# A sixth two-level product (M5), inner results as chains of sums in PSUM, and more weight splits on GpSimd, in a two-level Strassen MLP kernel

## The chip, the cores and the metric

The kernel runs on one core of one Trainium2 chip. The time is device time in microseconds (us), the median of several executions. The core has a tensor engine (TensorE, "PE" in the profile; "PEld" is its weight load), VectorE ("DVE"), ScalarE ("ACT"), GpSimd ("POOL"), SyncE ("SP"), which only issues transfers here, and 16 DMA engines. One profiled execution of each kernel gives the trace. Unless it is said otherwise, runs compared below are fast runs (the granted TensorE clock of the two main profiles is 0.99 or more).

## The reference

```python
# x: 8 x 1024 x 1024, w1: 1024 x 4096, w2: 4096 x 1024, all float32
h = x @ w1
h = 0.5 * h * (1 + np.tanh(np.sqrt(2 / np.pi) * (h + 0.044715 * h ** 3)))
return (h @ w2).astype(np.float32)
```

## The kernel before

The 8192 rows of x are worked on in eight super-blocks of 1024, SB0 to SB7. Each has two stages. "M-one" is x @ w1 with the GELU, as one level of Strassen-Winograd: seven products instead of eight, 448 matmuls of 512 columns, in float16 with float32 sums in PSUM. "M-two" is the second matmul, again seven products M1 to M7. Their operands are differences of blocks of g (the GELU's result) and sums of blocks of w2.

In SB0 and SB1 the sums of w1 and w2 are still being made, on chip, mostly by VectorE, and written to DRAM. From SB2 on they are loaded. There, M-two uses a second level: in the kernel before, M1, M2, M3, M6 and M7 are each seven smaller products (class `Inner`), and M4 and M5 stay one-level. A one-level product takes 64 matmuls of 512 columns, a two-level one 112 of 256.

The smaller products need their own weight sums, "splits". They are made once, during SB1 and SB2, either by VectorE (`split_jobs`) or by GpSimd (`split_on_pool`):

```python
def split_on_pool(m, h):                  # GpSimd: half h of product m's splits
    raw = []
    for k in range(2):
        raw.append(unit(2, HALF))         # a buffer of pool `up`
        nc.sync.dma_start(out=flat(raw[k]), in_=stored(w2_d[2*k+h], raw2_d[2*k+h], m))
    t = {}
    for n, (_, u, op, v) in W_SUMS.items():           # four sums
        if n % 2:
            two = unit(2, HALF)
        t[n] = two[:, (n + 1) % 2]
        ...
        nc.gpsimd.tensor_tensor(out=t[n], in0=in0, in1=in1, op=op)
        nc.gpsimd.dma_start(out=in_d[m][...], in_=t[n])
...
# in M-one, after block c of 16:
if sb == 2 and c < 8 and c % 2 == 0:
    split_on_pool(FROM_SUMS[c // 4], c // 2 % 2)      # FROM_SUMS = (1, 3)
```

So before, GpSimd makes splits only in SB2's M-one; M2's are made by VectorE in SB1's M-two.

The inner products are put together by VectorE, mostly with one copy and then sums that read PSUM:

```python
def steps(self, into):                    # class Inner; ab, bb, cb are PSUM banks
    self.multiply(1, ab, True);  act_copy(v, ab);              yield 1
    self.multiply(6, bb, True);  tt(c12, pair(v), pair(bb), ADD, True); ...; yield 2
    self.multiply(2, ab, False); act_copy(c11, pair(ab)); ...; yield 3
    self.multiply(7, bb, False); tt(c21, pair(v), pair(bb), ADD, True); ...; yield 4
    ...                                   # products 5, 4, 3
```

Work of VectorE that belongs to other products is put into slots of the PE sequence by a table, `FILL_2`: "27:a34 d21 d12" means that after step 7 of M2 three jobs are issued ("a" makes an operand, "x" a block difference, "d" and "e" are sums of outputs). The program pins these jobs of VectorE to their order, so a job that waits holds up those behind it (e4_fill below shows a stand of 5.23 us).

Two pools matter: `up` has 26 buffers of 4 KB per partition for everything (weights, differences, results), `gcp` has 4 for operands. A new tile gets the buffer that came free, and its first writer waits for that buffer's last reader.

## Time and profile before

| | before |
|---|---|
| time, median of 3 runs | 1528.55 us (1527.73 to 1528.93) |
| PE busy | 1517.1 of 1525.9 us (99%) |
| SB1: M-one, M-two | 96.91, 96.69 us |
| SB2: M-one, M-two | 96.82, 88.76 us |
| SB3 to SB6, each: M-one, M-two | 96.7, 88.75 us |

Stages are counted here and below from the first matmul of a stage to the first matmul of the next. First the page of the profile of before: its span and the busy time of each engine.

```profile
span 1525.9 us, 22990 instructions
PE 1517.1 (99%) x8702; PEld 852.3 (56%) x8702; DVE 1073.8 (70%) x1354; ACT 486.3 (32%) x817; POOL 357.2 (23%) x380
```

Next the chain of waits, that is the chain of work that ended last, in order of time, for SB3: start, duration, engine and line. Line 366 is M-one, 791 a one-level product of M-two, 726 the two-level ones.

```profile
594.78 96.69 PE ps L366 x448
691.48 13.81 PE ps L791 x64
705.29 36.68 PE ps L726 x336
741.97 13.81 PE ps L791 x64
755.78 24.45 PE ps L726 x224
```

PE waits for nobody here. A one-level product takes 13.81 us, a two-level one 36.68 / 3 = 12.23 us. The waits of PE in before, with total, number and longest in us:

```profile
PE ps L366 <- DVE tmp L142: 1.5, 2, 1.4
PE ps L366 <- DVE u L142: 1.4, 1, 1.4
...
PE ps L366 <- ACT tmp L430: 0.6, 1, 0.6
```

With the one line left out (1.2 us at the very start) they sum to 4.7 us, all before SB1's M-one is 4 us old. The kernel is bound by PE alone, and a new wait of PE has nothing to hide behind.

### The profile page before, as it was taken

The numbers are of one execution on the slowest core, as the hardware profiler recorded it, in microseconds if no ns is written. First come the engines' busy times: TensorE is split into PE (matmuls) and PEld (weight loads), VectorE is DVE, ScalarE is ACT, GpSimd is POOL, SyncE is SP. The second block draws the span as 40 slices with busy tenths as digits, with TensorE's granted clock in tenths as the row PEclk, the third lists the DMA queues.
The fourth block names the chain that finished last, engine by engine and source line by source line (L and its number), as shares of the span: only waits on it lengthen the run. The fifth ranks groups of instructions, "written<-read, shape, count | busy, mean of one in ns | idle before, by whom it ended". The sixth has DMA issues, their size and how long they took to land.

```text
span 1525.9 us, 22990 instructions
## 1 busy us (share of the span) xinstructions
PE 1517.1 (99%) x8702; PEld 852.3 (56%) x8702; DVE 1073.8 (70%) x1354; ACT 486.3 (32%) x817; POOL 357.2 (23%) x380
## 2 busy tenths in 40 slices
PE   9999999999999999999999999999999999999999
PEld 4444444444444677446764477544875448744486
DVE  5876868768755787557875587656876567855786
ACT  6655024410144212442124411344113441144300
POOL 1242011211297022130212203131121400204011
PEclk9999999999999999999999999999999999999999
DMA  9999985894998899769996699966999769993697
GB/s 317 348 327 349 253 281 184 281 304 156 351 362 232 309 324 312 240 159 328 321 305 212 176 348 320 312 186 198 329 308 325 185 211 320 306 353 90 221 326 185
DMA packets 226191, 417.84 MB, mean 274 GB/s; under 512 B 78752, under 2 KB 85920, under 8 KB 225184
## 3 DMA queue, kind: packets, MB, share of 16 engines
q1 hardware_dynamic: 193536, 314.64, 61.4%
q0 software_dynamic: 32544, 101.73, 24.4%
q8 instruction: 68, 1.11, 0.3%
q14 instruction: 43, 0.35, 0.1%
HBM read 311.43 MB, written 119.54 MB: 282 GB/s over the span
## 4 chain that ended last, share of the span: by engine, by line
PE 85%; DVE 0%; issue 0%
PE ps L366 44%; PE ps L726 24%; PE ps L791 17%; DVE u L142 0%
## 5 line engine op out<-in xcount | busy, mean ns | idle before, releaser
L366 PE MATMUL ps<-u 128*128 128x512 f16 x3584 | 776.1, 379 | 3.6 <-DVE tmp L142 1.5
L366 PEld LDWEIGHTS <-u 128*128 128x128 f16 x3584 | 350.5, 98 | 427.1 <-issue 4.7
L142 DVE TENSOR_TENSOR tmp<-tmp,ps 128x512 f32<-128x512 f32 x528 | 361.7, 686 | 298.1 <-ACT tmp L430 114.6
L376 ACT ACTIVATE g<-tmp 128x512 f16<-128x512 f32 x256 | 161.1, 630 | 294.4 <-DVE tmp L142 294.3
L726 PE MATMUL ps<-u,gc 128*128 128x256 f16 x1920 | 224.3, 273 | 0.0
L142 DVE TENSOR_TENSOR u<-u 128x2048 f16<-128x2048 f16 (+3 forms) x233 | 211.9, 937 | 16.6 <-ACT u L321 11.7
L791 PE MATMUL ps<-u,gc 128*128 128x512 f16 x1024 | 222.6, 379 | 0.0
L726 PEld LDWEIGHTS <-gc 128*128 128x128 f16 x1920 | 187.9, 98 | 21.7
L376 ACT ACTIVATE g<-ps 128x512 f16<-128x512 f32 x256 | 151.4, 596 | 88.1 <-PE ps L366 87.9
L791 PEld LDWEIGHTS <-gc 128*128 128x128 f16 x1024 | 100.1, 98 | 119.6
L791 PE MATMUL ps<-u,g 128*128 128x512 f16 x640 | 139.8, 379 | 0.0
L490 POOL DMA_DIRECT2D out_dram<-u x58 | 58.5, 1019 | 311.2 <-DVE u L142 299.0
L142 DVE TENSOR_TENSOR u<-u,ps 128x512 f32<-128x512 f32 x131 | 89.7, 685 | 46.1 <-PE ps L791 17.0
L158 ACT COPY tmp<-ps 128x512 f32<-128x512 f32 x54 | 31.6, 585 | 272.1 <-PE ps L726 161.3
L469 POOL TENSOR_TENSOR u<-g,g 128x2048 f16<-128x2048 f16 x24 | 97.2, 4067 | 75.0 <-ACT g L376 60.1
L791 PEld LDWEIGHTS <-g 128*128 128x128 f16 x640 | 62.7, 98 | 75.5
L726 PE MATMUL ps<-u,g 128*128 128x256 f16 x864 | 103.1, 273 | 0.0
L478 POOL DMA_DIRECT2D out_dram<-u x52 | 39.0, 770 | 249.0 <-ACT u L158 227.3
L430 ACT COPY tmp<-ps 128x512 f32<-128x512 f32 x128 | 72.9, 569 | 69.7 <-PE ps L366 69.7
L142 DVE TENSOR_TENSOR tmp<-ps,tmp 128x512 f32<-128x512 f32 x128 | 88.3, 690 | 5.9 <-PE ps L366 1.2
L726 PEld LDWEIGHTS <-g 128*128 128x128 f16 x864 | 84.5, 98 | 11.1
L142 DVE TENSOR_TENSOR u<-tmp,ps 128x512 f32<-128x512 f32 x60 | 41.3, 688 | 63.9 <-PE ps L726 41.4
(42 smaller groups left out, 736.2 us busy)
## 6 DMA issues: line engine op xcount, KB each, us to landing
u<-w_d SPq DMA_DIRECT2D x384, 256.0 KB, 7.2
u<-in_d SPq DMA_DIRECT2D x120, 512.0 KB, 7.3
u<-raw_d SPq DMA_DIRECT2D x132, 256.0 KB, 6.6
out_dram<-u POOLq DMA_DIRECT2D x58, 512.0 KB, 9.0
u<-raw_d SPq DMA_DIRECT2D x56, 512.0 KB, 7.1
gc<-in_w_dram SPq DMA_DIRECT2D x48, 512.0 KB, 6.5
w_d<-u POOLq DMA_DIRECT2D x36, 512.0 KB, 4.2
raw_d<-u SPq DMA_DIRECT2D x32, 512.0 KB, 9.9
```

What stands on the lines that cost most here:

```text
L142: i = nc.vector.tensor_tensor(out=out, in0=in0, in1=in1, op=op)
L158: tc.keep_in_program_order(nc.scalar.copy(out=out, in_=in_))
L366: nc.tensor.matmul(bank, lhsT=ops[:, k, :], rhs=xs[m][:, k, :], start=(first and k == 0), stop=(k == KH - 1), skip_group_check=not first,)
L376: gelu_last[0] = nc.scalar.activation(out=g[b][:, c, :], in_=src, func=GELU)
L430: nc.scalar.copy(out=v, in_=pb)
L469: nc.gpsimd.tensor_tensor(out=early[m][b], in0=gu, in1=gv, op=SUB)
L478: return nc.gpsimd.dma_start(out=out2[r0:r0 + P, o0:o0 + OH], in_=src, **kw)
L490: return nc.gpsimd.dma_start(out=rows, in_=src, **kw)
L726: tc.keep_in_program_order(nc.tensor.matmul(bank[:, i * OH // 2:(i + 1) * OH // 2], lhsT=t[:, c, i * P:(i + 1) * P], rhs=self.y[j][:, c, : ...
L791: i = nc.tensor.matmul(pair(bank), lhsT=a[:, c, :], rhs=chunks(pieces[c // QC])[:, :, c % QC, :], start=(first and c == 0), stop=(c == NI ...
```

## The change

M5 becomes two-level as well, which takes PE work away. To have VectorE carry it, the inner results are rewritten: products 1, 6, 7 and 4 add up in one PSUM bank, and after each of the four ScalarE copies the sum so far into the result; VectorE adds the rest. Output block 12, which is M3 + M5 and was added by an accumulating store, is added on chip ("f" jobs). The splits of M2 and M5 are made by GpSimd in SB1's M-one. GpSimd's splits take their buffers from `gcp` now and no longer from `up`, in SB1 and in SB2, and SB2's are spread over blocks 0, 3, 6 and 9 instead of 0, 2, 4 and 6. GpSimd also makes two more block differences (M6's, `EARLY`) at the end of each M-one from SB2 on. Left out of the cuts below: a turned sign in the fourth weight sum, and differences that are now written over one of their operands.

```diff
-FROM_2 = (2,)
-FROM_SUMS = (1, 3)
-INNER = MADE_INNER + FROM_2 + FROM_SUMS
+ON_POOL = {1: (2, 5), 2: (1, 3)}
+INNER = MADE_INNER + ON_POOL[1] + ON_POOL[2]
...
-EARLY = ((1, "11"), (1, "21"), (2, "11"), (2, "21"))
-W_ORDER = (1, 6, 2, 7, 5, 4, 3)
+EARLY = ((1, "11"), (1, "21"), (2, "11"), (2, "21"), (6, "11"), (6, "21"))
+W_ORDER = (1, 2, 6, 5, 7, 3, 4)
...
-    ;12:a21;14:a22;15:a23;17:a24
-    ;21:u0 u1;22:a31;23:u2 u3;24:a32;25:a33 d11;26:d22;27:a34 d21 d12
-    ;32:g50;34:g51 e11;35:g52 e22;36:e21;37:g53 e12
-    ...
+    ;11:x522;13:a21;14:a22;15:a23;16:a24;17:x521
+    ;21:u0 u1;23:a31 u2;24:a32;25:a33;26:a34;27:u3 x511
+    ;31:x512;32:d11;33:a51;34:a52;35:a53;36:a54;37:d22 d21 d12
+    ;51:e11 e22;53:a61 e21;54:a62;55:a63;56:a64;57:e12 x721
+    ...
-            if sb == 2 and c < 8 and c % 2 == 0:
-                split_on_pool(FROM_SUMS[c // 4], c // 2 % 2)
+            if sb in ON_POOL and c < 12 and c % 3 == 0:
+                split_on_pool(ON_POOL[sb][c // 6], c // 3 % 2)
...
-        if sb:
-            for m in FROM_2:
-                for job in split_jobs(m, lambda: pieces(m)):
-                    job()
...
-            raw.append(unit(2, HALF))
+            raw.append(gcp.tile([P, 2, HALF], DT, name="gc"))
...
-                two = unit(2, HALF)
+                two = gcp.tile([P, 2, HALF], DT, name="gc")
...
-            self.multiply(1, ab, True)
-            v = temp()
-            act_copy(v, ab)
-            ...
+            for n, (j, bank, first, out, adds) in enumerate((
+                (1, a, True, "11", ()),
+                (2, b, True, None, ("11",)),
+                (6, a, False, "12", ()),
+                (5, c, True, None, ("12",)),
+                (7, a, False, "22", (("22", c),)),
+                (3, b, True, None, ("12",)),
+                (4, a, False, "21", ()),
+            ), 1):
+                self.multiply(j, bank, first)
+                if out is not None:
+                    t = quarter(into, out)
+                    if self.base is None:
+                        act_copy(t, pair(bank))
+                    else:
+                        tt(t, quarter(self.base, out), pair(bank), ADD, True)
+                for o in adds:
+                    ...
+                    tt(t, t, pair(ps), ADD, True)
+                ...
+                yield n
...
-            3: Inner(3, g, out("12")),
-            6: Inner(6, g, out("22", accum_op=ADD)),
+            3: Inner(3, g),
+            5: Inner(5, g),
+            6: Inner(6, g, out("22", accum_op=ADD), x=early[6]),
...
+                elif kind == "m":
+                    add(u2, 5, b, SUB)
+                    ...
+                elif kind == "f":
+                    add(into[3], 5, b, ADD)
+                    if b in ("22", "12"):
+                        store_rows(sb, "12", a, into[3][a])
```

Product 6 adds onto bank a, so it may not start before ScalarE has copied bank a after product 1. Only product 2 (16 matmuls, 1.75 us) lies between, so a copy that is late by more than about 1 us stops PE.

More of the change, by code (lines that the diff above doesn't have):

```diff
@@ L65 @@
 W_TERMS = {1: "11", 2: "21", 3: "22"}
-W_SUMS = {1: (5, "12", SUB, "11"), 2: (6, "22", SUB, 1), 3: (7, "22", SUB, "12"), 4: (4, 2, SUB, "21")}
+W_SUMS = {1: (5, "12", SUB, "11"), 2: (6, "22", SUB, 1), 3: (7, "22", SUB, "12"), 4: (4, "21", SUB, 2)}
 S_TERMS = {1: "11", 2: "12", 4: "22"}
 S_SUMS = {1: (5, "21", ADD, "22"), 2: (6, 1, SUB, "11"), 3: (7, "11", SUB, "21"), 4: (3, "12", SUB, 2)}
-EARLY = ((1, "11"), (1, "21"), (2, "11"), (2, "21"))
-W_ORDER = (1, 6, 2, 7, 5, 4, 3)
+EARLY = ((1, "11"), (1, "21"), (2, "11"), (2, "21"), (6, "11"), (6, "21"))
+W_ORDER = (1, 2, 6, 5, 7, 3, 4)
 def slots(table):
     return {(int(k[0]), int(k[1])): v.split() for k, v in (row.split(":") for row in table.split(";"))}
-FILL_2 = slots("""00:x122 x112 a11 a12 a13 a14 x222 x212 x622 x612 x621 x611
-    ;12:a21;14:a22;15:a23;17:a24
-    ;21:u0 u1;22:a31;23:u2 u3;24:a32;25:a33 d11;26:d22;27:a34 d21 d12
-    ;32:g50;34:g51 e11;35:g52 e22;36:e21;37:g53 e12
-    ;50:a61 x721;51:a62 x722;52:a63 x711;53:a64 x712
-    ;64:a71;66:a72;67:a73;71:a74;72:n5;73:n1;74:n2;75:n7;76:n6""".replace("\n    ", ""))
+FILL_2 = slots("""00:x122 x112 a11 a12 a13 a14 x222 x212 x622 x612
+    ;11:x522;13:a21;14:a22;15:a23;16:a24;17:x521
+    ;21:u0 u1;23:a31 u2;24:a32;25:a33;26:a34;27:u3 x511
+    ;31:x512;32:d11;33:a51;34:a52;35:a53;36:a54;37:d22 d21 d12
+    ;51:e11 e22;53:a61 e21;54:a62;55:a63;56:a64;57:e12 x721
+    ;61:x722 x711;62:x712 m11;63:a71;64:a72;65:a73 m22;66:a74;67:m21 m12
+    ;71:f11 f12;72:f21 f22;73:n5;74:n1;75:n2;76:n7;77:n6""".replace("\n    ", ""))
 @with_exitstack
@@ L279, in __init__, with make @@
             self[3], self[4] = blocks["11"], blocks["22"]
-        def make(self, *ms, cols=slice(None), pin=False):
+        def make(self, *ms, cols=slice(None), pin=False, over=False):
             for m in ms:
@@ L284, in make @@
                 if m not in self:
-                    self[m] = unit(KH, HT)
+                    self[m] = self.blocks[u] if over and m in IN_PLACE else unit(KH, HT)
                 tt(self[m][:, :, cols], self.blocks[u][:, :, cols], self.blocks[v][:, :, cols], SUB, pin)
@@ L387, in matmul1 @@
         xb = [None]
-        early = {1: {}, 2: {}}
+        early = {1: {}, 2: {}, 6: {}}
         blocks = None
@@ L464, in matmul1 @@
                     x_transpose(xb[0], load_in_order, blocks, range((c - 9) // 2, (c - 7) // 2))
-            if sb > 1 and c >= NI - 4:
-                m, b = EARLY[c - NI + 4]
-                early[m][b] = unit(NI // 2, HT // 2)
+            if sb > 1 and c >= NI - len(EARLY):
+                m, b = EARLY[c - NI + len(EARLY)]
                 gu, gv = (inner_block(g[t], b) for t in A_TERMS[m])
+                early[m][b] = gu if m in IN_PLACE else unit(NI // 2, HT // 2)
                 nc.gpsimd.tensor_tensor(out=early[m][b], in0=gu, in1=gv, op=SUB)
@@ L597, in prepare @@
             ops[i] = operand2(g, m, q, True)
-        fill = [lambda m=m: xs.make(m, pin=True) for m in (5, 1, 2, 7, 6)]
+        fill = [lambda m=m: xs.make(m, pin=True, over=True) for m in (5, 1, 2, 7, 6)]
         if sb:
@@ L735, in steps @@
         def steps(self, into):
-            base = self.base
-            c11, c12, c21, c22 = (quarter(into, b) for b in ("11", "12", "21", "22"))
-            if base is not None:
-                b11, b12, b21, b22 = (quarter(base, b) for b in ("11", "12", "21", "22"))
-            ab, bb, cb = psum(), psum(), psum()
-            self.multiply(1, ab, True)
-            v = temp()
-            act_copy(v, ab)
-            yield 1
-            self.multiply(6, bb, True)
-            tt(c12, pair(v), pair(bb), ADD, True)
@@ L748, in steps @@
-            if base is not None:
-                tt(c12, c12, b12, ADD, True)
-            yield 2
-            self.multiply(2, ab, False)
-            if base is None:
-                act_copy(c11, pair(ab))
-            else:
-                tt(c11, b11, pair(ab), ADD, True)
-            self.part("11", c11)
-            yield 3
-            self.multiply(7, bb, False)
-            tt(c21, pair(v), pair(bb), ADD, True)
-            if base is not None:
-                tt(c22, c21, b22, ADD, True)
-                tt(c21, c21, b21, ADD, True)
@@ L763, in steps @@
-            yield 4
-            self.multiply(5, cb, True)
-            tt(c22, c21 if base is None else c22, pair(cb), ADD, True)
-            self.part("22", c22)
-            yield 5
-            self.multiply(4, ab, True)
-            tt(c21, c21, pair(ab), SUB, True)
-            self.part("21", c21)
-            self.rows(1, into[1])
-            yield 6
-            self.multiply(3, cb, False)
-            tt(c12, c12, pair(cb), ADD, True)
-            self.part("12", c12)
-            self.rows(0, into[0])
@@ L777, in steps @@
-            yield 7
+            a, b, c = psum(), psum(), psum()
+            for n, (j, bank, first, out, adds) in enumerate((
[15 more added lines that the diff above has]
+                for o in adds:
+                    o, ps = o if isinstance(o, tuple) else (o, bank)
+                    t = quarter(into, o)
+                    tt(t, t, pair(ps), ADD, True)
+                for o, at in (("11", 2), ("22", 5), ("12", 6), ("21", 7)):
+                    if n == at:
+                        self.part(o, quarter(into, o))
+                if n > 5:
+                    self.rows(n - 6, into[n - 6])
+                yield n
@@ L821, in matmul2 @@
         end = sb == NSB - 1
-        ops, pieces = {}, {}
         u2, u = halves()
@@ L838, in matmul2 @@
             products[7] = Inner(7, g, out("11", accum_op=ADD))
-        def copy(q, ps):
-            t = temp()
-            act_copy(t, ps)
-            return t
         def post4(q, ps):
@@ L847, in post4, with add @@
             store(sb, "21", q, u[q])
-        def post5(q, ps):
-            store(sb, "12", q, copy(q, ps), accum_op=ADD)
-            tt(u[q], u[q], ps, SUB, True)
-            if not end:
-                store(sb, "11", q, u[q])
-        posts = {4: post4, 5: post5}
-        def load(m):
-            if m in products:
-                products[m].load()
-            else:
-                pieces[m] = load_pieces(m)
+        def add(o, m, b, op):
+            t = quarter(o, b)
+            tt(t, t, quarter(into[m], b), op, True)
         def run(key):
             for job in FILL_2.get(key, ()):
-                kind, m, i = job[0], int(job[1]), job[2:]
+                kind, b = job[0], job[1:]
+                m, i, a = int(b[0]), b[1:], int(b[0]) - 1
                 if kind == "x":
@@ L869, in run @@
                     products[m].make(int(i))
-                elif kind == "g":
-                    ops[m, int(i)] = operand2(g, m, int(i), True)
                 elif kind == "u":
                     tt(u[m], u[m], rows[1][m], ADD, True)
-                elif kind in "de":
-                    b = job[1:]
-                    d = quarter(into[1], b)
-                    tt(d, d, quarter(into[2 if kind == "d" else 3], b), SUB if kind == "d" else ADD, True)
-                    if job in ("e21", "e12"):
-                        a = int(b[0]) - 1
-                        store_rows(sb, "22", a, into[1][a])
+                elif kind == "d":
+                    add(into[1], 2, b, SUB)
+                elif kind == "e":
+                    add(into[1], 3, b, ADD)
+                    if b in ("21", "12"):
+                        store_rows(sb, "22", a, into[1][a])
+                elif kind == "m":
+                    add(u2, 5, b, SUB)
+                    if b in ("21", "12") and not end:
+                        store_rows(sb, "11", a, u2[a])
+                elif kind == "f":
+                    add(into[3], 5, b, ADD)
+                    if b in ("22", "12"):
+                        store_rows(sb, "12", a, into[3][a])
                 elif nxt is not None:
-                    nxt.make(m, pin=True)
+                    nxt.make(m, pin=True, over=True)
         order = (4, 1, 2, 3, 5, 6, 7)
-        load(4)
+        pieces = load_pieces(4)
         run((0, 0))
@@ L888, in matmul2 @@
             if after is not None:
-                load(after)
+                products[after].load()
             if m in products:
@@ L896, in matmul2 @@
                 ps = psum()
-                a = ops.get((m, q))
-                matmuls2(ps, operand2(g, m, q) if a is None else a, pieces[m], True, pin=True)
-                posts[m](q, ps)
-                run((m, q))
+                matmuls2(ps, operand2(g, m, q), pieces, True, pin=True)
+                post4(q, ps)
     idle = consts.tile([P, HT], DT, name="idle")
```

## The prediction

> **What bounds the kernel.** TensorE. The page gives PE 99% busy, and the chain of waits is PE almost alone from 219 us to the end. Every super-block from the third on costs 185.44 us: M-one 448 matmuls of 512 columns in 96.69 (215.8 ns each), M4 and M5 64 each in 13.81, the five two-level products 112 of 256 columns each in 12.23 (109.2 ns). PE's whole idle time is under 4 us (groups of instructions). Any new wait of PE costs in full.
>
> **Removed.** M5 goes from 64 matmuls of 512 columns (13.81) to 112 of 256 (12.23): 1.58 us in each of six super-blocks, 9.5 us, all on the critical path. That alone gives 1519.
>
> **Added or moved, off the path if it fits.** VectorE, per second stage: about +2 sums of f16 128x2048 (1.14 apart) and +3 f32 sums (0.6): about 76 us of 87. ScalarE: 10 more copies of 0.585 us; it is nearly empty there. DMA (0.95 to 1.08 busy there): +1.6 MB of M5 weights, about -1 MB of block-12 stores: neutral. GpSimd: two more 4.07 us differences per super-block, in M-one, where it idles. The split of M2's weights leaves VectorE (8 sums, 4.9 us in SB1's M-two: no PE wait there, no gain).
>
> **New waits of PE.**
> 1. M3. In the built order, ScalarE's first copy out of M3's bank a goes into a buffer at the SBUF address of the weights of M3's second product: pool `up` (26 buffers) is full, and a load of M5's weights takes the buffer freed by product 1. The copy thus waits for product 2's end, and product 3, which adds onto bank a, waits for the copy. Elsewhere one product (1.75 us) lies between. Cost: 0.04 + 0.585 + about 0.1 = 0.7 us, in five super-blocks (not the last, where no next x holds buffers): +3.6 us.
> 2. SB1. The raw splits (16 sums of 2.13 us on GpSimd) now run about 212 to 250 us, beside VectorE's f16 sums of w1. The Trainium skill, "SBUF — State Buffer", section "Who interferes with whom", says that a VectorE instruction with two SBUF inputs and a GpSimd instruction reading SBUF contend, and one blocks wholly. The trace agrees: next to GpSimd casts that began first, VectorE sums of 1.22 took up to 1.85. A pair of w1 sums leaves PE about 1 us of slack (bank r's sum ends at 237.87, product 7 begins at 238.96). Estimate: +1.5 us (0 to 5) over SB1.
> 3. The rest looks safe: weight loads are released at least 14 us of PE time before use and land in 7 (15 at most); M5's first copy waits for M2's accumulating store, 15.7 us ahead, which takes 9 to 12.
>
> **Sum.** 1528.5 - 9.5 + 3.6 + 1.5 = 1524. Range 1519 to 1529. Chances: faster by over 2% 0.01, same 0.98, slower 0.01.
>
> **What would show it.** Chain of waits: M5 12.23. A PE wait for ScalarE's copy of about 0.7 us at M3's third product, five times, none in the last super-block. Super-block 185.44 to about 184.6. SB1's M-one over 96.5, with VectorE f16 sums above 1.22 us and PE waiting for VectorE. SB0, and each M-one from SB2 on, unchanged.
>
> **What would make it wrong.** The M3 copy waiting for something else or not at all (then 1520); the port conflict costing nothing or much more; DMA, already full in the second stage, landing weights or M2's store late; VectorE backlog reaching the next M-one.

## The result, and the profile after

The changed kernel takes 1547.01 us (median of 4 runs, 1545.61 to 1549.39), beside 1528.14 us for before in the same rounds. The ratio is 1.0124 (95% interval 1.0107 to 1.0142). Ratios here are the mean time of one kernel's fast runs over that of the other's of the same rounds, so they are not quite the ratio of the medians quoted. The change is within 2%, but slower by some 19 us, where 4.5 us less had been predicted. It lies far outside the range (1519 to 1529).

The page of the profile after, same lines:

```profile
span 1547.6 us, 23826 instructions
PE 1514.1 (98%) x8990; PEld 880.8 (57%) x8990; DVE 1105.3 (71%) x1376; ACT 519.6 (34%) x874; POOL 421.9 (27%) x386
```

PE is busy 3.0 us less, yet the span is 21.7 us longer: PE waits more. The largest waits of PE:

```profile
PE ps L366 <- DVE tmp L142: 15.6, 12, 5.8
PE ps L722 <- ACT u L158: 7.5, 10, 0.8
PE ps L773 <- DMA u<-w_d: 2.5, 2, 2.3
...
```

Three are new: for VectorE in M-one (15.6), for ScalarE in the two-level products (7.5, ten times), for DMA in front of a one-level product (2.5). By stage, from first matmul to first matmul:

| stage | before | after | difference |
|---|---|---|---|
| start and SB0, to the start of SB1's M-one | 215.44 | 216.92 | +1.48 |
| SB1 M-one | 96.91 | 111.17 | **+14.26** |
| SB1 M-two | 96.69 | 96.69 | 0 |
| SB2 M-one | 96.82 | 100.17 | **+3.35** |
| SB2 M-two | 88.76 | 91.00 | **+2.24** |
| SB3 to SB6, each M-one + M-two | 185.45 | 185.70 | +0.25, four times |
| SB7 M-one + M-two, to its last matmul | 185.35 | 184.21 | −1.14 |

The rows sum to 1.48 + 14.26 + 3.35 + 2.24 + 1.00 − 1.14 = 21.2 us, the difference of the two profiled executions up to their last matmuls; the other 0.5 us of the 21.7 lies behind those. The profiled one of after is the slowest of its four, so this is somewhat more than the 18.9 us between the medians. The first row is not the change: SB0's M-one took between 98.8 and 101.1 us in the profiles, with the same code.

**SB3 to SB6.** The chain of waits of after in SB3, to be held against that of before above:

```profile
616.11 96.69 PE ps L366 x448
712.80 13.81 PE ps L773 x64
726.62 27.96 PE ps L722 x256
754.60 0.59 ACT u L158
755.20 0.04 issue
755.24 12.40 PE ps L722 x112
767.67 0.09 DVE u L142
767.83 0.59 ACT u L158
768.42 0.04 issue
768.46 33.35 PE ps L722 x304
```

The removed time is real, since M5 runs on line 722 now. But the chain leaves PE twice for a ScalarE copy: at 754.60 in M3 and at 767.83 in M5. The starts of the matmuls on either side, 109 ns apart otherwise, are 946 ns apart at the first place and 1107 to 1111 at the second, in each of SB2 to SB6. This makes 0.84 + 1.00 = 1.84 us, against the 1.58 that M5 saves: +0.26, as the table has it (+0.25). SB7 has neither wait, and there the saving shows, less 0.44 us that I did not follow up.

The second wait was not foreseen. The timeline of after around it (start, duration; in brackets the idle time before and what ended it):

```profile
765.86 3.09 DVE L142 TENSOR_TENSOR u<-u 128x512 f32<-128x512 f32 x5
...
767.83 0.58 ACT L158 COPY u<-ps 128x512 f32<-128x512 f32 x1 [3.07 <-DVE u L142]
...
768.46 0.38 PE L722 MATMUL ps<-u,gc 128*128 128x256 f16 x2 [0.84 <-ACT u L158]
```

The copy is M5's first, of product 1, which had ended at about 765.7. It waits for VectorE, not for PE. By the buffer assignment of the built program, its target has the buffer of M2's result, whose last reader is job d12. That is the last of three "d" jobs of slot 37, which start at 765.86 behind an operand sum of 1.22 us. The third ends at 767.75, and 0.08 us later the copy starts. M2's two stores to DRAM, which read the same result, had been issued at 750.95 and 751.99 and landed at 762.34 and 765.57, so the copy didn't wait for them.

**SB1's M-one.** The timeline of before, two w1 sums of VectorE:

```profile
233.72 2.35 DVE L142 TENSOR_TENSOR u<-u 128x2048 f16<-128x2048 f16 x2
```

And the timeline of after at the same place, with GpSimd's splits and PE:

```profile
236.03 8.85 DVE L142 TENSOR_TENSOR u<-u 128x2048 f16<-128x2048 f16 x2
...
236.39 4.21 POOL L665 TENSOR_TENSOR gc<-gc 128x1024 f16<-128x1024 f16 x2
...
240.53 1.11 POOL L666 DMA_DIRECT2D in_d<-gc  x2
...
241.66 2.13 POOL L665 TENSOR_TENSOR gc<-gc 128x1024 f16<-128x1024 f16 x1
...
245.53 1.01 PE L366 MATMUL ps<-u 128*128 128x512 f16 x2 [5.82 <-DVE tmp L142]
```

Two VectorE sums take 8.85 us instead of 2.35: the first 5.65 us and the second 3.27, each of 1.22 when undisturbed. The first ends 1.1 us after GpSimd's run of two sums does, and the second 1.1 us after the third sum, each about one undisturbed sum later. PE waits for the PSUM sums behind them. In this stage 6 of the 21 such sums that start in it are held (1.59, 3.14, 3.14, 3.23, 3.27 and 5.65 us), none in before. Not every overlap holds VectorE: a sum at 249.74 runs beside GpSimd's for 1.14 us and takes 1.22. There it is GpSimd's sum, begun 0.08 us later, that takes longer: 3.12 us instead of 2.13. After its gap of 6.2 us from start to start PE is also slow: the next matmuls start 427 ns apart instead of 216, until 249.3. The trace has the granted clock at 0.5 from 242.77 to 249.59. The sums by engine over this stage show both, first before, then after (columns: stretch, length, busy time of PE, PEld, DVE, ACT and POOL with instruction counts, granted clock, DMA share, GB/s).

```profile
215.44:312.35 96.91, 96.86 (x450) 43.82 (x449) 76.52 (x101) 44.15 (x78) 16.18 (x31) 1.00 0.71 240
```

```profile
216.92:328.09 111.17, 99.97 (x450) 44.29 (x449) 90.01 (x103) 44.26 (x78) 59.50 (x63) 0.97 0.83 295
```

PE's idle time goes from 96.91 − 96.86 = 0.05 to 111.17 − 99.97 = 11.20 us, and its busy time for the same matmuls grows by 3.11 us: 11.15 + 3.11 = 14.26. Of the 3.11, counted from start to start, 2.0 us are the matmuls at the halved clock; the rest stands at the waits, where the last matmul before the gap counts as busy to its (modelled) end. VectorE is busy 13.5 us more with nearly the same instructions.

**SB2.** The chain of waits of before there:

```profile
409.20 96.82 PE ps L366 x448
506.02 13.81 PE ps L791 x64
```

And that of after:

```profile
429.71 91.76 PE ps L366 x425
521.47 4.70 DMA u<-w_d
526.17 0.04 issue
526.21 14.71 PE ps L773 x60
```

M4's weights come late. Their loads were issued at 520.85, 96.1 us after the stage began, and before had issued them at 492.06, 83.0 us after. The 60 matmuls take 14.71 us, since the first of them again run 427 ns apart (up to 529.5). The granted clock is 0.5 for 3.41 us from 526.07, although PE had waited only 2.27 us for the first weights and 0.24 us for the next. This makes about 2.3 of the 3.35 us; the other 1.0 is a shorter wait of PE for VectorE, 4.9 us after the stage began, to which e9_all_but_sb2 comes back.

### The profile page after: what moved, and what is told of

It is laid out like the page before. It is cut to its first block, busy times and chain, and to the rows that moved or that the text cites. A ratio compares the mean times of both kernels' runs of the same rounds, so it can differ in the third digit from the quotient of the medians.

```text
span 1547.6 us, 23826 instructions
## 1 busy us (share of the span) xinstructions
PE 1514.1 (98%) x8990; PEld 880.8 (57%) x8990; DVE 1105.3 (71%) x1376; ACT 519.6 (34%) x874; POOL 421.9 (27%) x386
## 4 chain that ended last, share of the span: by engine, by line
PE 81%; DVE 2%; issue 1%; ACT 0%; DMA 0%; DVEq 0%; ACTq 0%
PE ps L366 42%; PE ps L722 28%; PE ps L773 12%; DVE u L142 1%; DVE tmp L142 1%; ACT u L158 0%; DMA u<-w_d 0%; DVE g L142 0%; DVE gc L142 0%; ACT g L376 0%; DVEq L142 0%; ACTq L158 0%
## 5 line engine op out<-in xcount | busy, mean ns | idle before, releaser
L366 PE MATMUL ps<-u 128*128 128x512 f16 x3584 | 779.1, 380 | 17.2 <-DVE tmp L142 15.6
L366 PEld LDWEIGHTS <-u 128*128 128x128 f16 x3584 | 350.9, 98 | 443.1 <-issue 22.6
L722 PE MATMUL ps<-u,gc 128*128 128x256 f16 x2304 | 257.5, 273 | 7.7 <-ACT u L158 7.5
L142 DVE TENSOR_TENSOR u<-u 128x512 f32<-128x512 f32 (+3 forms) x270 | 250.1, 959 | 16.8 <-ACT u L321 11.9
L158 ACT COPY u<-ps 128x512 f32<-128x512 f32 x164 | 96.0, 585 | 423.8 <-PE ps L722 316.5
L490 POOL DMA_DIRECT2D out_dram<-u x68 | 66.6, 1176 | 404.0 <-DVE u L142 355.5
L142 DVE TENSOR_TENSOR u<-u,ps 128x512 f32<-128x512 f32 x164 | 111.9, 682 | 40.6 <-PE ps L773 16.4
L773 PE MATMUL ps<-u,gc 128*128 128x512 f16 x640 | 138.8, 379 | 0.0
L722 PE MATMUL ps<-u,g 128*128 128x256 f16 x864 | 99.2, 273 | 0.0
L722 PE MATMUL ps<-u 128*128 128x256 f16 x864 | 99.2, 273 | 0.0
L142 DVE TENSOR_TENSOR u<-g,g 128x2048 f16<-128x2048 f16 x48 | 57.5, 1220 | 48.7 <-PE ps L722 44.5
L722 PEld LDWEIGHTS <-u 128*128 128x128 f16 x864 | 84.6, 98 | 11.1
```

The source lines that it names most:

```text
L142: i = nc.vector.tensor_tensor(out=out, in0=in0, in1=in1, op=op)
L158: tc.keep_in_program_order(nc.scalar.copy(out=out, in_=in_))
L366: nc.tensor.matmul(bank, lhsT=ops[:, k, :], rhs=xs[m][:, k, :], start=(first and k == 0), stop=(k == KH - 1), skip_group_check=not first,)
L490: return nc.gpsimd.dma_start(out=rows, in_=src, **kw)
L722: tc.keep_in_program_order(nc.tensor.matmul(bank[:, i * OH // 2:(i + 1) * OH // 2], lhsT=t[:, c, i * P:(i + 1) * P], rhs=self.y[j][:, c, : ...
L773: i = nc.tensor.matmul(pair(bank), lhsT=a[:, c, :], rhs=chunks(pieces[c // QC])[:, :, c % QC, :], start=(first and c == 0), stop=(c == NI ...
```

## The experiments

The theory after this reading has three parts. (A) SB1: GpSimd sums that read SBUF hold VectorE's sums of two SBUF tiles, which is what the Trainium skill describes in "SBUF — State Buffer", section "Who interferes with whom": such a VectorE instruction contends with a GpSimd instruction that reads SBUF, not with one that only writes it. This is called the port conflict below. The rival: the extra loads and stores, GpSimd's queue or the four `gcp` buffers delay VectorE. (B) SB2: the splits' new buffers (`gcp` instead of `up`) delay the chain of jobs behind which M4's weights are loaded. Rivals: the lateness comes from SB1, or from the two more early differences on GpSimd. (C) SB2 to SB6: the copies wait for buffers, and another order of jobs frees them in time.

Nine kernels were run. All gave right results but e2_memset, which is wrong on purpose. The texts of what was expected speak of about 107 us for SB1's M-one. That was an estimate made before the table above, which has 111.2. e2_memset and e7_gap were run once each; both have a granted clock of 1.00, and the reading rests on their stage times.

### e1_sb1_dve: M2's and M5's splits on VectorE, in SB1's M-two

```diff
-ON_POOL = {1: (2, 5), 2: (1, 3)}
-INNER = MADE_INNER + ON_POOL[1] + ON_POOL[2]
+ON_POOL = {2: (1, 3)}
+INNER = MADE_INNER + (2, 5) + ON_POOL[2]
 # in SB1's M-two, before product 4:
+if sb:
+    for job in split_jobs(2, lambda: pieces(2)):
+        job()
 # and among its fill jobs:
+fill = split_jobs(5, lambda: pieces(5)) + split_jobs(7, ...) + ...
```

> The changed kernel, but the weight splits of M2 and M5 are made by VectorE in SB1's second stage (M2's before product 4 as in the kernel before, M5's four during product 2); no split runs on GpSimd in SB1. Theory (the splits on GpSimd in SB1 hold up VectorE's f16 sums, and PE with them): SB1's M-one falls from about 107 us to 96.7, no f16 sum of VectorE in it is above 1.3 us, PE's idle time before L366 falls from 17 to about 4 us, total about 1547 - 13 = 1534. Rival (the loss is from w1's larger wait for DMA or cold matmuls by chance): SB1's M-one stays over 103. SB2's start of M4 stays late (the same code), super-blocks from SB3 on stay at 185.7.

Measured: 1531.89 us (1531.83 to 1532.75, 4 runs), ratio to before 1.0025 (1.0010 to 1.0040). SB1's M-one takes 96.90 us, as before, and no f16 sum in it is over 1.222 us. SB1's M-two stays at 96.7, so VectorE has room for M5's eight sums beside M2's, which it had before. SB2 is still late (99.00 and 90.22), with PE waiting 1.04 us for M4's weights, and SB3 to SB6 are still 89.00. Its chain of waits in SB1's M-one is PE alone, from 4 us after its start:

```profile
219.65 93.18 PE ps L366 x431
```

So the 14.3 us go with the GpSimd splits, and SB2's lateness is not only SB1's.

### e2_memset: GpSimd writes as long, but doesn't read

```diff
+if blank:                                 # SB1 only; the result is wrong on purpose
+    for _ in range(3):
+        nc.gpsimd.memset(t[n], 0.0)
+    nc.gpsimd.tensor_tensor(out=t[n][:, :32], in0=in0[:, :32], in1=in1[:, :32], op=op)
+else:
     nc.gpsimd.tensor_tensor(out=t[n], in0=in0, in1=in1, op=op)
```

> Wrong result on purpose. The changed kernel, but each of SB1's 16 split sums on GpSimd is replaced by three memsets of the same output and a sum of its first 32 columns: the loads, buffers, queues, stores and about the same busy time of GpSimd stay, but it hardly reads SBUF. Theory (two engines that read SBUF contend for the port): VectorE's f16 sums in SB1 are at 1.22 us but for rare ones held under 0.3 us, SB1's M-one about 97, total about 1534. Rival (GpSimd's queue order, the four gc buffers, or the DMA traffic of the splits cost the time, not the reading): SB1's M-one stays above 103 us and PE still waits for VectorE there.

Measured: 1531.28 us, one run, relative error 0.82 as intended. SB1's M-one takes 96.90 us. The loads, stores, buffers and the place in GpSimd's queue are as in after, and GpSimd is busy even longer (three writes of 0.97 us and a short sum, against 2.13). Its timeline, with the same two VectorE sums and GpSimd beside them:

```profile
234.84 0.97 POOL L667 MEMSET gc<- 128x1024 f16 x1
...
235.15 2.35 DVE L142 TENSOR_TENSOR u<-u 128x2048 f16<-128x2048 f16 x2
...
238.32 2.75 POOL L667 MEMSET gc<- 128x1024 f16 x3
```

Nine of the 21 sums in the stage overlap memsets, by 0.3 to 1.4 us. Eight of them take 1.22 us as ever. The ninth (1.265) and one other (1.355), which is the longest, also overlap one of the short sums that still read. This agrees with the statement of the Trainium skill quoted above: here GpSimd's writing didn't hold VectorE, and its reading did. The rival of part A falls.

### e7_gap: the same GpSimd sums, never directly behind one another

The 5.65 us pose a question: a sum that waits for one GpSimd sum should take at most about 2.13 + 1.22 = 3.35 us. A memset, which doesn't read, was put before each GpSimd sum in SB1, and the order was pinned.

```diff
+if gap:                                   # SB1 only
+    tc.keep_in_program_order(nc.gpsimd.memset(t[n], 0.0))
-nc.gpsimd.tensor_tensor(out=t[n], in0=in0, in1=in1, op=op)
+i = nc.gpsimd.tensor_tensor(out=t[n], in0=in0, in1=in1, op=op)
+if gap:
+    tc.keep_in_program_order(i)
```

> The changed kernel, but in SB1 each of GpSimd's 16 split sums has a memset (about 0.97 us, writes only) ahead of it, kept in order, so that no two sums of GpSimd follow each other at once. Theory (a VectorE sum that finds the port taken gets it only when GpSimd has no further reading instruction directly behind, which is why one took 5.65 us over two GpSimd sums): no f16 sum of VectorE in SB1 takes more than 1.22 + 2.13 = 3.4 us, and SB1's M-one is clearly below the 107 us, about 100 to 103. Rival (a VectorE sum waits for any number of GpSimd sums whatever stands between): sums over 4 us stay, M-one about 107.

Measured: 1536.49 us, one run. SB1's M-one takes 102.15 us. Five sums are held, at 1.49, 2.27, 2.69, 2.90 and 3.07 us, so none beyond 3.35. In its timeline, the two sums of the example above (2.69 and 1.21):

```profile
234.04 3.83 DVE L142 TENSOR_TENSOR u<-u 128x2048 f16<-128x2048 f16 x2
```

Nearly as many collisions, each over with the one GpSimd sum that it met, cost less. This doesn't show why one sum of after was held across two. Sums of GpSimd directly behind one another aren't enough for it: in after itself the VectorE sum of 271.13 met two in a row (271.00 and 273.15) and took 3.14 us, so it had its turn after the first, and the second took 3.11 us instead of 2.13. In the five kernels that have the long hold (5.24 to 5.65 us: after, e3_sb2_up, e4_fill, e6_fill2, e8_before_pool2), the records of the VectorE sum and of the first GpSimd sum begin within 0.4 us of each other, VectorE's first in four of the five; in e7_gap every held sum begins at least 0.14 us after GpSimd's. What decides stays open. The pinning also spreads the splits over a longer time (their last ends at 301.9 instead of 280.0), so the 9 us of difference in the stage are not all owed to the shorter holds.

### e8_before_pool2: the kernel before, with one split moved

```diff
 # open kernel: before
+if sb == 1 and c in (0, 3):
+    split_on_pool(2, c // 3, True)        # with gcp buffers
-if sb:
-    for m in FROM_2:
-        for job in split_jobs(m, lambda: pieces(m)):
-            job()
```

> The kernel before with one part of the change alone: M2's weight split moves from VectorE (SB1's second stage) to GpSimd in SB1's M-one, with gc buffers; M5 stays one-level. Theory (the port costs by itself, without the second level): VectorE f16 sums up to 3 to 5.7 us in SB1, M-one of SB1 about 103 instead of 96.5, total 1528 + 4 to 9 = 1532 to 1537. Rival (the cost needs M5's extra loads or splits): 1528 to 1530.

Measured: 1537.49 us (1531.97 to 1538.61, 4 runs) beside 1528.2, ratio 1.0053 (1.0037 to 1.0069). In its profile, which is of the slowest run, SB1's M-one takes 106.58 us, two sums that start in it are held for 5.59 and 3.27 us, and PE waits accordingly (waits of PE):

```profile
PE ps L366 <- DVE tmp L142: 8.7, 4, 5.8
```

So the part of the change that moves splits into SB1's M-one costs 8 to 10 us by itself, with nothing else of it present, and half of the splits are enough. The runs differ by 6.6 us, more than those of any other kernel here: the fastest has a granted clock of 1.000, the other three 0.998. That fewer sums met in it is likely, but it was not profiled.

### e3_sb2_up: SB2's split buffers from `up` again

```diff
-split_on_pool(ON_POOL[sb][c // 6], c // 3 % 2)
+split_on_pool(ON_POOL[sb][c // 6], c // 3 % 2, sb == 2)
 # in split_on_pool, for raw and two:
+def new():
+    return unit(2, HALF) if in_up else gcp.tile([P, 2, HALF], DT, name="gc")
```

> The changed kernel, but SB2's splits (M1, M3) take their buffers from pool up (26) as in the kernel before, not from gc (4); SB1's stay in gc. Theory (four gc buffers serialize load, sum and store of a split on GpSimd, which in its order holds up the casts of the next x, then the transposes on the DMA queue, then M4's weights): the fourth cast mark on GpSimd comes about 30 us earlier, M4's weights are issued before about 510 us of the profile's time instead of 520.9, PE's wait for them (2.3 us, with slow matmuls after it) is gone, total 1547 - 4 = 1543. Rival (M4's weights are late because of the two more early differences on GpSimd, which end at 517): unchanged 1547.

Measured: 1542.69 us (1541.94 to 1542.86, 4 runs), ratio 1.0093 (1.0078 to 1.0108). SB1 is as in after (111.10), SB2's M-one is 96.82 and its M-two 89.01, and PE no longer waits for M4's weights. Their loads are issued 90.4 us after the stage's start. The expectation that the jobs ahead of them would come some 30 us earlier was wrong (the fourth of the x casts that the loads wait behind comes 58.5 us into the stage, against 63.2 in after and 49.2 in before): a few microseconds are enough. The rival with the two more early differences falls, since they are still there. The rival with SB1's lateness falls too, at least as a sufficient cause, since SB1 is as late as in after. e8_before_pool2 says the same from the other side: its SB1 is late by 9.7 us, and M4's loads of SB2 are issued 82.8 us into the stage, as in before (83.0).

### e4_fill: another order of the jobs, first try

```diff
-    ;21:u0 u1;23:a31 u2;24:a32;25:a33;26:a34;27:u3 x511
-    ;31:x512;32:d11;33:a51;34:a52;35:a53;36:a54;37:d22 d21 d12
+    ;21:u0 u1;23:a31 u2;24:a32;25:a33;26:a34;27:u3
+    ;31:d11 d12;32:d22 x511;33:d21 a51;34:a52;35:x512 a53;36:a54
```

> The changed kernel, but with the fill table's order changed: x511 and x512 are made two and four steps later, the four d jobs (into M1's result) earlier. By the built order, M3's first copy then no longer takes the buffer of product 2's weights, and M5's first copy no longer takes the buffer that the last d job frees. Theory (these two buffers cost 0.7 and 0.9 us of PE in five super-blocks, and nothing else costs there): each super-block from SB3 to SB6 takes 183.9 us instead of 185.70 (before: 185.44), PE has no wait for ScalarE's copy, total 1547 - 8 = 1539. Rival (the second level of M5 loads VectorE or DMA so much that a wait appears elsewhere): 185 or more.

Measured: 1551.83 us (1550.46 to 1552.78, 4 runs), ratio 1.0156 (1.0139 to 1.0173). A miss. The two waits for copies are gone, but M5's block x511 got the buffer of M2's result instead, which a store to DRAM was still reading (timeline, VectorE; between the two lines it did nothing):

```profile
563.79 0.69 DVE L142 TENSOR_TENSOR u<-u 128x512 f32<-128x512 f32 x1
569.71 1.23 DVE L142 TENSOR_TENSOR u<-g,g 128x2048 f16<-128x2048 f16 x1 [5.23 <-DMA out_dram<-u]
```

The store was issued at 559.49 and landed at 569.62, 10.1 us later. VectorE takes its work in order and stood still for 5.23 us, and PE then waited for VectorE 12.1 us in five places. Freeing a buffer early is no use if the next writer is one whose wait costs more.

### e6_fill2: another order, second try

```diff
-    ;21:u0 u1;23:a31 u2;24:a32;25:a33;26:a34;27:u3 x511
-    ;31:x512;32:d11;33:a51;34:a52;35:a53;36:a54;37:d22 d21 d12
+    ;21:u0 u1;23:a31 u2;24:a32;25:a33;26:a34;27:u3
+    ;31:x511;32:x512;33:a51 d22;34:a52 d21;35:a53 d11;36:d12 a54
```

> The changed kernel with the third fill table alone (as in e5_all). Theory (M3's and M5's copy waits cost 0.7 and 0.9 us, and e4_fill failed only because its x511 took the buffer of M2's result while that was being stored, so that VectorE stood for 5 us): super-blocks SB3 to SB6 take 183.9 us instead of 185.70, no PE wait for ScalarE's copy, SB1 and SB2 as slow as in the changed kernel, total 1547 - 9 = 1538. Rival (moving the x's makes VectorE late whatever the buffer): 185.5 or more.

Measured: 1536.67 us (1535.13 to 1538.19, 4 runs) beside 1528.2, ratio 1.0058 (1.0043 to 1.0073). Every M-two from SB3 to SB6 takes 87.17 us, the super-block 183.87: 1.83 less than in after, the 1.84 of the two gaps. PE has no wait for ScalarE's copies left, and the chain of waits has the six two-level products of SB3 in one piece:

```profile
719.58 73.36 PE ps L722 x672
```

Part C holds. SB1's M-one is 110.49, as it should be with the splits left on GpSimd.

### e5_all: the three repairs together

The edits of e1_sb1_dve, e3_sb2_up and e6_fill2.

> The changed kernel with three repairs together: M2's and M5's splits made by VectorE in SB1's second stage, SB2's splits in buffers of pool up, and a third fill table (x511 and x512 one and four steps later, before the d jobs; all d jobs done by M3's sixth product), in which by the built order no copy of ScalarE waits for a late buffer and no x takes one whose store is still out. Theory (the loss is the sum of the port, the gc buffers in SB2 and the two copy waits; the second level of M5 itself pays its 1.58 us in each of six super-blocks): super-blocks from SB2 on take 183.9 us, total 1528 - 9.5 = 1518.5 to 1520. Rival (with the second level the second stage is too full for VectorE or the DMA): 1524 or more, with waits in M5 or M6.

Measured: 1519.74 us (1518.77 to 1520.45, 5 runs) beside 1528.2 (9 runs), ratio 0.9944 (0.9931 to 0.9956). It beats both kernels, before by 0.6%, clear of the noise but within the 2% that counts as the same. Its profiled span is 1516.6 us, with PE 99% busy. Its chain of waits in SB3 (line 728 is the two-level products, M5 among them):

```profile
592.85 96.69 PE ps L366 x448
689.55 13.81 PE ps L779 x64
703.36 73.36 PE ps L728 x672
```

Six two-level products take 73.36 us without a break, 12.23 each. SB1's M-one is 96.90, SB2 is 96.82 and 87.17, and SB3 to SB6 are 96.7 and 87.17. Five M-twos save 1.59 us and SB7's saves 1.18, so 9.1 us; the medians differ by 8.5.

### e9_all_but_sb2: the repairs without the one of SB2

The edits of e1_sb1_dve and e6_fill2; SB2's splits keep their `gcp` buffers.

> e5_all, but SB2's splits are back in the four gc buffers, as in the change. It measures the loss in SB2 alone, in an otherwise repaired kernel. Theory (the four gc buffers make M4's weights late): a PE wait for the DMA of M4's weights at the end of SB2's M-one and slow matmuls after it, SB2's two stages together 2 to 5 us over e5_all's 184.0, total 1522 to 1525. Rival (SB2 was late only because SB1's splits ran late in it): equal to e5_all, 1519.7.

Measured: 1521.91 us (1520.51 to 1522.66, 4 runs) beside 1528.46, ratio 0.9957 (0.9942 to 0.9972). SB2's M-one is 97.79 and its M-two 87.17. PE does not wait for M4's weights, so part B in its simple form, the `gcp` buffers alone, falls. What remains of it is a gap of 1.3 us early in SB2's M-one, where PE waits for VectorE: the first split of SB2 runs beside VectorE's last f16 sums (four of them take 3.91 us together, where the next four take 2.48), and with `up` buffers (e3_sb2_up, e5_all) there is no such gap. That this is the port conflict again is read from the trace, not tried. The whole set of runs shows how near the edge the weights are. The middle column is the time from the start of SB2's M-one to the issue of M4's weight loads:

| kernel | issued after, us | from issue to M4's first matmul, us | PE waits at M4's first matmul |
|---|---|---|---|
| before | 83.0 | 13.8 | no |
| e5_all (`up`) | 89.4 | 7.5 | no |
| e3_sb2_up (`up`) | 90.4 | 6.4 | no |
| e9_all_but_sb2 | 92.3 | 5.5 | no |
| e2_memset | 93.2 | 4.5 | no (0.28 us a little later) |
| e4_fill | 93.8 | 4.0 | no (three of 0.2 to 0.3 us a little later) |
| e7_gap | 94.0 | 4.4 | 0.49 |
| e6_fill2 | 94.2 | 4.2 | 0.45 |
| e1_sb1_dve | 95.0 | 4.1 | 1.04 |
| after | 96.1 | 4.1 | 2.27 |

In the kernels that wait, the first weights can be used about 4.1 us after the issue, so before had a lead of nearly 10 us (13.8 less 4.1), and the change used up more than that. The buffers in `gcp` are worth 2.9 us (e9_all_but_sb2 against e5_all) to 5.7 us (after against e3_sb2_up). SB1's lateness is worth about 1 us (after against e1_sb1_dve: 96.1 and 95.0) or nothing (e8_before_pool2). How the rest, the 6.4 us from before to e5_all, splits between the job table, the spacing of the splits and GpSimd's queue stays open; the runs change these together.

## Why the prediction was right or wrong

**Right: what bounds the kernel and what M5 saves.** PE, and 1.58 us per super-block. e5_all and e6_fill2 show 87.17 instead of 88.75 us.

**Right: M3's copy.** Predicted 0.7 us in five super-blocks, none in the last; measured five gaps of 946 ns instead of 109, so 0.84 each, 4.2 us in all, none in SB7.

**Right: the loads of VectorE and DMA in M-two.** Predicted about 76 us for VectorE's second stage; measured 75.2 of 89.0 in SB3's M-two (72.8 of 88.75 before), with the DMA share 0.96 where it had been 1.00.

**Wrong: "The rest looks safe: ... M5's first copy waits for M2's accumulating store, 15.7 us ahead".** The copy was late in each of SB2 to SB6, by VectorE and not by the store. It cost 1.00 us five times, 5.0 us. The step took the store for the last reader of the buffer that the copy writes, and so left out job d12. In PE's time slot 37 lies before M5, but its jobs stand in VectorE's queue behind an operand sum, and three run one behind another. The slot says when a job is issued, not when it is done. e6_fill2 moved the jobs earlier and the wait was gone.

**Wrong in size: step 2, SB1's port conflict, "+1.5 us (0 to 5)".** The mechanism was right, and e1_sb1_dve, e2_memset and e8_before_pool2 bear it out. The term measured +14.26 us. The estimate had taken the worst from a place where VectorE's 1.22 us had become 1.85, beside a cast of 1.03 us. A sum of 2.13 us held VectorE longer (up to 3.27 us), and once two in a row did: 5.65 us, and not 1.85. The estimate also left out that PE runs at half rate afterwards: 2.0 of the 14.26 us. The Trainium skill has this in "TensorE: Matmul & The Clock Gate", Part 1: an idle array drops to half its clock and needs about 3.4 us of work to come back. The trace agrees in kind: after the wait of 5.82 us it has 427 ns between starts instead of 216 for 3.8 us.

**Wrong: "SB0, and each M-one from SB2 on, unchanged".** SB2's M-one was +3.35 us and M4 behind it slow, 2.0 us beyond the 0.25 that its M-two shares with SB3. The sentence "weight loads are released at least 14 us of PE time before use" failed with it: in SB2, M4's were issued 4.1 us before use (13.8 in before). SB2 differs from the later super-blocks in that the splits' sums and x's casts share GpSimd's queue. e3_sb2_up shows that the `gcp` buffers of the splits decide it in the changed kernel; alone they were not enough for this wait (e9_all_but_sb2).

Put together: −9.5 (M5) + 0.4 (SB7) + 4.2 (M3's copy) + 5.0 (M5's copy) + 14.3 (SB1) + 3.35 + 2.0 (SB2) + 1.5 (SB0, noise) = 21.2 us of the profiled pair. Predicted was −9.5 + 3.6 + 1.5 = −4.4.

## What to carry to other kernels

Before giving work to an engine "that idles", look at what the other engines do at that moment. GpSimd was nearly idle in SB1's M-one (busy 16 of 97 us), but VectorE was summing pairs of SBUF tiles there, and a sum of 1.22 us became one of 5.65 with PE waiting behind it; the kernel before did its GpSimd splits in SB2, where VectorE has no such sums in M-one, and lost nothing. When a result is released by a job of an in-order engine, count that engine's whole queue in front of it. And when several buffers come free in turn, ask who takes each one: e4_fill repaired two waits of 1 us and made one of 5.

## What the Trainium skill lacked or had wrong

- "SBUF — State Buffer", section "Who interferes with whom", has the rule right (two SBUF inputs on VectorE against a GpSimd instruction that reads SBUF). It says, of VectorE's two-port modes, that whoever issues first gets the shared ports for the whole instruction; if that holds for these sums too, one would expect a hold of at most one GpSimd sum: 2.13 + 1.22 = 3.35 us. What the page doesn't say is who goes next when GpSimd has a second sum directly behind the first. Here a waiting VectorE sum was held across both in one place (5.65 us in after, 5.59 in e8_before_pool2), and in another it went between them (3.14 us, and GpSimd's second sum took 3.11). With a memset between the sums no VectorE sum took over 3.07 us (e7_gap). In the 5.65 us case VectorE's record even begins 0.36 us before GpSimd's; whether a record begins when the instruction is issued or when it gets its ports, these traces don't tell.
- The same section gives no cost for the engines behind. Here 11.15 us of PE's idle time came of it in one stage of 97 us.
- "TensorE: Matmul & The Clock Gate", section "Back-to-back issue gap", gives about 131 ns per matmul of 512 columns as the sustained figure with weight loads. Here 448 such matmuls, each with a weight load, run 215.8 ns apart for a whole stage (96.69 us), which is the section's figure for an isolated matmul (about 216), and those of 256 columns run 109.2 ns apart.
- No page that I used gives a time for a store that adds to what is in DRAM, while the queues are full: M2's took 10.1 us from issue to landing (e4_fill), and its source buffer was blocked as long.
